# Low parts of the gate and up matrices: every piece, not every second one, by a second load that adds

## The chip, the core and the metric

The kernel runs on one core of a Trainium2 chip. TensorE (PE) does the matrix products, VectorE (DVE) and ScalarE (ACT) work on elements, GpSimd (POOL) and SyncE (SP) mostly issue DMAs here. 16 DMA engines move data between the chip's memory (DRAM) and the core's on-chip memory. DMAs issued by SP and by POOL stand in two different queues, q1 and q0 of the profile, and are served by the same 16 engines. The metric is device time of one execution in microseconds; lower is better.

## What is computed

One decoder layer over 256 tokens with 2048 channels, in float32: three token mixers, a SwiGLU block, a per-layer input embedding and a final norm. What matters here is the SwiGLU block:

```python
D_FF = -(-8 * D_MODEL // (3 * 256)) * 256        # 5632
...
        h = rms_norm(x, g_ffn[i])
        gate, up = jnp.split(h @ w_gate_up[i], 2, axis=-1)
        x = x + (jax.nn.silu(gate) * up) @ w_down[i]
```

The matrix `w_gate_up` has 2048 rows and 11264 columns, 92 MB in float32. It is used once, so the whole of it is streamed through the core.

## The kernel before

**Products in split form.** PE is fed with numbers of type float32r. To keep float32's accuracy, each operand is split in a high part (the value rounded to float32r) and a low part (the value less its high part), and each product is the sum of three: high by high, high by low, low by high (lines 255 to 257, function `products`). The tokens' side is split once; the weights are split as they arrive.

**Groups, chunks, pieces.** A `Group` is a block of 512 columns of one matrix with all its rows. `run(plan)` cuts it into `Chunk`s of 4 row blocks of 128, and a chunk has 2 pieces of 2 row blocks: 128 partitions by 2 by 512 numbers, 512 KB. Per piece PE does 2 row blocks by 2 halves of the tokens by 3 products: 12, so 24 for a chunk.

**Gate and up.** The plan has 11 column blocks `j`, for each a gate group and an up group of 16 row blocks, so 4 chunks each: 22 groups, 88 chunks, 176 pieces. They run in two parts, blocks 0 to 4 and blocks 5 to 10 (`CUT = 5`, line 964); after each part come the groups of `w_down` that use its results. Between chunks stand the evacuations: `ev_gate` (sigmoid on ACT, product on DVE), `ev_up` (product on DVE), and, two chunks later, the transposes of the result (line 324).

**The way of a piece.** `issue` (line 165) loads it into a buffer `raw` (a pool of 5) from SP. `split_w` makes its parts `whi` and `wlo` (pools of 5 each). It does so for the chunk after the one whose products come next in program order. For most pieces `split` copies `raw` to `whi` on ACT (line 111), rounding it, and subtracts on DVE: `wlo = raw - whi` (line 112). In the gate and up matrices the second piece of a chunk (`a == 1`) goes another way: ACT copies `raw` to `whi` (line 189) and writes the negated `whi` to `wlo` (line 190), and POOL issues a DMA (line 192) that loads the same 512 KB from DRAM a second time and adds it to `wlo` in place. So that piece is fetched twice, and DVE does nothing for it.

**What sets the order.** Each engine works through its own instructions in program order and waits on semaphores of the others. A piece's `whi` and `wlo` come free when PE has done the 12 products of the piece five before it. A `raw` buffer comes free when its last reader is done: DVE's subtraction, or ACT's copy where a second load is used. `c.ins` only places work of the mixers (`advance`), of which none is left in this stage.

Of the kernel before, what the change touches and what calls it, by code (L numbers as in the profile page):

```python
# [64 lines left out]
def kernel(  # L65
# [19 lines left out]
    def nm(s):  # L85
        uid[0] += 1
        return f"{s}_{uid[0]}"

    def big(name, shape=(P, 8, T), dt=F32):
        return t8.tile(list(shape), dt, tag="t8", name=nm(name))  # L90
# [19 lines left out]
    def split(hi, lo, src):  # L110
        a = act.activation(out=hi, in_=src, func=AF.Copy)  # L111
        b = dve.tensor_tensor(out=lo, in0=src, in1=hi.bitcast(F32), op=ALU.subtract)  # L112
        return a.ins, b.ins
# [59 lines left out]
    def split_w(c):  # L173
        c.parts = []
        if c.g.kind == "hold":
            b = big("whold", (P, 2, 4, c.g.n), F32R)
        for a, r in enumerate(c.raw):
            if c.g.kind == "hold":
                hi, lo = (b[:, q, 2 * a : 2 * a + 2, :] for q in range(2))
            else:  # L180
                hi = wparts.tile([P, 2, c.g.n], F32R, tag="whi", name=nm("whi"))
                lo = wparts.tile([P, 2, c.g.n], F32R, tag="wlo", name=nm("wlo"))
            if c is chunks[0]:
                for q in range(2):
                    c.g.pre([2 * a + q])
                    split(hi[:, q, :], lo[:, q, :], r[:, q, :])
            elif c.g.w is w_gu_v and a == 1:

                act.activation(out=hi, in_=r, func=AF.Copy)  # L189
                neg = act.activation(out=lo, in_=hi.bitcast(F32), func=AF.Copy, scale=-1.0)  # L190
                k = c.ks[2]
                nc.gpsimd.dma_start(  # L192
                    out=lo, in_=c.g.w[:, k : k + 2, c.g.c0 : c.g.c0 + c.g.n], accum_op=ALU.add
                )
                c.ins = (neg.ins, c.ins[1])
            else:
                c.ins = split(hi, lo, r)
            c.parts.append((hi, lo))
# [62 lines left out]
    def run(plan):  # L261
# [3 lines left out]
        while now[0] < len(chunks):  # L265
# [5 lines left out]
            while state["split"] < min(len(chunks), i + PREF_SPLIT):  # L271
                split_w(chunks[state["split"]])
                state["split"] += 1
# [77 lines left out]
    w_in_v, w_gu_v, w_dn_v = wv(w_in), wv(w_gate_up), wv(w_down)  # L351
# [757 lines left out]
```

## Time and profile before

| | us |
|---|---|
| median of 2 runs | 1913.3 (1912.48 to 1914.11) |
| the profiled execution, in all | 1915.16 |
| its span in the profile | 1913.4 |
| gate and up, first part (40 chunks) | 224.64 |
| `w_down`, first part | 109.7 |
| gate and up, second part (48 chunks) | 267.87 |

The profile shows one execution. Engines are named PE, PEld (PE's loading of the stationary operand, beside its products), DVE, ACT, POOL, SP. A group's row reads: line, engine, operation, output<-inputs, shape, count, then busy time and mean duration in ns of one, then the idle time just before them and who ended it. A row of the view of stretches reads: from:to, length, busy time and number of instructions of PE, PEld, DVE, ACT and POOL, then PE's granted clock (1.00 is full), the mean share of time in which the 16 DMA engines had a packet (above 1 where packets overlap), and GB/s. A row of a DMA queue reads: packets, MB, share of the 16 engines' time. A row of DMA issues ends with the median time in us from issue to landing. A row of waits reads: in total, how often, the longest. A row of the timeline reads: start, duration, engine, line, operation. A product's duration holds its way through the array; how fast PE goes is read from the distance of the starts.

### The profile page before, as it was taken

Reading aid. Unit: us, or ns where it says so; the run is one execution under the profiler, and the core shown is the slowest. Engines: PE = TensorE matmul, PEld = TensorE weight load, DVE = VectorE, ACT = ScalarE, POOL = GpSimd, SP = SyncE. Lnnn points to the kernel's source line nnn. Section 1 sums busy time; section 2 is a strip of 40 time slices with the busy share of each in tenths; the row PEclk is TensorE's granted clock in tenths of the full one; section 3 lists DMA queues with packets and bytes.
Section 4 is the critical chain, followed back from the end, with each engine's and each line's share of the span. In section 5 each row is a group of like instructions: output and inputs, shape, how many; then the busy total and the mean of one; then the engine's idle time right before and its main releaser. Section 6 shows DMA issues by size and latency. Waiting matters only on the chain.

```text
span 1913.4 us, 25619 instructions
## 1 busy us (share of the span) xinstructions
PE 1895.4 (99%) x9958; PEld 1633.6 (85%) x9958; DVE 1110.1 (58%) x1359; ACT 1001.5 (52%) x1122; POOL 115.0 (6%) x110
## 2 busy tenths in 40 slices
PE   8999999999999999999999999999999999999998
PEld 8988889999998888888888888888888888888887
DVE  8558776667888889765555332235433233355565
ACT  6466466544344444644445666653356666544554
POOL 1000000000000000000000122210012222100000
PEclk9999999999999999999999999999999999999999
DMA  8756556555666656676665999996699999966563
GB/s 276 219 168 199 175 176 185 161 156 172 179 185 198 193 165 211 194 239 188 209 191 185 255 289 275 275 280 193 191 262 284 277 288 280 274 187 191 183 187 122
DMA packets 213914, 407.41 MB, mean 213 GB/s; under 512 B 12976, under 2 KB 21808, under 8 KB 213664
## 3 DMA queue, kind: packets, MB, share of 16 engines
q1 hardware_dynamic: 188960, 356.02, 58.4%
q0 software_dynamic: 24832, 49.75, 14.6%
q8 instruction: 78, 1.28, 0.3%
q14 instruction: 44, 0.36, 0.1%
HBM read 403.62 MB, written 2.10 MB: 212 GB/s over the span
## 4 chain that ended last, share of the span: by engine, by line
PE 94%; DMA 3%; issue 1%; DVE 1%; ACT 0%; SPq 0%; POOLq 0%; DVEq 0%
PE acc L256 25%; PE acc L257 25%; PE acc L255 25%; PE acc L250 5%; PE acc L248 5%; PE acc L249 5%; DMA wlo<-in_w_gate_up_dram 2%; PE tr L324 1%; PE sc L546 1%; DMA x<-in_x_feat_dram 1%; DVE wlo L112 0%; DVE cv L105 0%; DMA raw<-in_w_in_dram 0%; DVE rw L734 0%; PE ov L617 0%
## 5 line engine op out<-in xcount | busy, mean ns | idle before, releaser
L112 DVE TENSOR_TENSOR wlo<-raw,whi 128x1024 fp32r<-128x1024 f32 (+2 forms) x590 | 705.7, 1199 | 694.0 <-ACT whi L111 693.2
L111 ACT ACTIVATE whi<-raw 128x1024 fp32r<-128x1024 f32 (+2 forms) x590 | 612.5, 1040 | 719.7 <-PE acc L257 508.9
L256 PE MATMUL acc<-wlo,xhi 128*128 128x512 f32 (+1 forms) x832 | 321.5, 386 | 2.2 <-DMA wlo<-in_w_gate_up_dram 2.1
L255 PE MATMUL acc<-whi,xhi 128*128 128x512 f32 (+1 forms) x832 | 321.3, 386 | 0.0
L257 PE MATMUL acc<-whi,xlo 128*128 128x512 f32 (+1 forms) x832 | 320.5, 385 | 0.0
L248 PE MATMUL acc<-hhi,whi 128*128 128x256 f32 x896 | 255.7, 285 | 5.3 <-ACT whi L111 5.1
L255 PE MATMUL acc<-whi,hhi 128*128 128x512 f32 (+1 forms) x672 | 255.6, 380 | 0.0
L250 PE MATMUL acc<-hhi,wlo 128*128 128x256 f32 x896 | 254.5, 284 | 0.9 <-DVE wlo L112 0.9
L257 PE MATMUL acc<-whi,hlo 128*128 128x512 f32 (+1 forms) x672 | 254.8, 379 | 0.0
L256 PE MATMUL acc<-wlo,hhi 128*128 128x512 f32 (+1 forms) x672 | 254.7, 379 | 0.0
L249 PE MATMUL acc<-hlo,whi 128*128 128x256 f32 x896 | 254.3, 284 | 0.0
L256 PEld LDWEIGHTS acc<-wlo,xhi 128*128 128x128 f32 x832 | 156.3, 188 | 36.7 <-DMA wlo<-in_w_gate_up_dram 6.1
L255 PEld LDWEIGHTS acc<-whi,xhi 128*128 128x128 f32 x832 | 156.3, 188 | 31.0
L257 PEld LDWEIGHTS acc<-whi,xlo 128*128 128x128 f32 x832 | 156.3, 188 | 30.8
L248 PEld LDWEIGHTS acc<-hhi,whi 128*128 128x128 f32 x896 | 172.8, 193 | 5.9 <-ACT whi L111 5.5
L250 PEld LDWEIGHTS acc<-hhi,wlo 128*128 128x128 f32 x896 | 172.6, 193 | 1.3 <-DVE wlo L112 1.3
L249 PEld LDWEIGHTS acc<-hlo,whi 128*128 128x128 f32 x896 | 172.9, 193 | 0.4 <-issue 0.2
L189 ACT ACTIVATE whi<-raw 128x1024 fp32r<-128x1024 f32 x88 | 93.3, 1061 | 134.1 <-PE acc L257 134.1
L257 PEld LDWEIGHTS acc<-whi,hlo 128*128 128x128 f32 x672 | 126.1, 188 | 23.6
L255 PEld LDWEIGHTS acc<-whi,hhi 128*128 128x128 f32 x672 | 126.2, 188 | 23.4
L256 PEld LDWEIGHTS acc<-wlo,hhi 128*128 128x128 f32 x672 | 126.2, 188 | 23.3
L192 POOL DMA_DIRECT2D wlo<-in_w_gate_up_dram x88 | 105.9, 1203 | 640.5 <-ACT wlo L190 583.1
(268 smaller groups left out, 2230.6 us busy)
## 6 DMA issues: line engine op xcount, KB each, us to landing
raw<-in_w_in_dram SPq DMA_DIRECT2D x262, 512.0 KB, 3.7
raw<-in_w_gate_up_dram SPq DMA_DIRECT2D x176, 512.0 KB, 5.9
wlo<-in_w_gate_up_dram POOLq DMA_DIRECT2D x88, 512.0 KB, 7.6
raw<-in_w_down_dram SPq DMA_DIRECT2D x88, 512.0 KB, 3.8
raw<-in_w_gla_out_dram SPq DMA_DIRECT2D x32, 512.0 KB, 3.7
raw<-in_w_o_dram SPq DMA_DIRECT2D x32, 512.0 KB, 3.7
raw<-in_w_ple_gate_dram SPq DMA_DIRECT2D x24, 512.0 KB, 4.1
raw<-in_w_sc_out_dram SPq DMA_DIRECT2D x16, 512.0 KB, 4.3
```

What stands on the lines that cost most here:

```text
L111: a = act.activation(out=hi, in_=src, func=AF.Copy)
L112: b = dve.tensor_tensor(out=lo, in0=src, in1=hi.bitcast(F32), op=ALU.subtract)
L189: act.activation(out=hi, in_=r, func=AF.Copy)
L192: nc.gpsimd.dma_start(out=lo, in_=c.g.w[:, k : k + 2, c.g.c0 : c.g.c0 + c.g.n], accum_op=ALU.add)
L248: pe.matmul(o, lhsT=whi[:, ms], rhs=shi, start=st and m % 2 == 0, stop=False)
L249: pe.matmul(o, lhsT=whi[:, ms], rhs=slo, start=False, stop=False)
L250: pe.matmul(o, lhsT=wlo[:, ms], rhs=shi, start=False, stop=sp and m % 2 == 1)
L255: pe.matmul(o, lhsT=shi[:, hs], rhs=whi, start=st, stop=False)
L256: pe.matmul(o, lhsT=shi[:, hs], rhs=wlo, start=False, stop=False)
L257: pe.matmul(o, lhsT=slo[:, hs], rhs=whi, start=False, stop=sp)
L324: pe.transpose(b[:, q, h * P : h * P + P], src[:, h, (j + q) * P : (j + q) * P + P], ident,)
L546: pe.matmul(b[:, e, :], lhsT=K[:, dt, :], rhs=Q[:, dt, :], start=q == 0, stop=q == 1)
```

## The change

The condition that picks the second piece of a chunk falls, so the first piece is made in the same way. The row block that the second load reads is now `c.ks[2 * a]`, 0 or 2 blocks into the chunk.

```diff
-            elif c.g.w is w_gu_v and a == 1:
+            elif c.g.w is w_gu_v:
 
                 act.activation(out=hi, in_=r, func=AF.Copy)
                 neg = act.activation(out=lo, in_=hi.bitcast(F32), func=AF.Copy, scale=-1.0)
-                k = c.ks[2]
+                k = c.ks[2 * a]
                 nc.gpsimd.dma_start(
                     out=lo, in_=c.g.w[:, k : k + 2, c.g.c0 : c.g.c0 + c.g.n], accum_op=ALU.add
                 )
-                c.ins = (neg.ins, c.ins[1])
+                c.ins = (neg.ins, neg.ins)
```

All else is as it was: the first load of every piece, the pools, the products. In 88 chunks one subtraction on DVE goes, and one copy on ACT and one DMA of 512 KB from POOL come.

ACT, some four chunks into the first part, before. The numbers behind the names tell buffers apart; DMAHW, DMASW, PE, DVE and Activation are the semaphores of SP's loads, of POOL's loads and of the engines:

```order
L111 ACTIVATE whi_9658<-raw_9617 128x1024 [waits DMAHW6_49,PE_49]
L189 ACTIVATE whi_9662<-raw_9619 128x1024 [waits DMAHW7_49,PE_49]
L190 ACTIVATE wlo_9663<-whi_9662 128x1024 [waits Activation_49]
L111 ACTIVATE whi_9700<-raw_9654 128x1024 [waits DMAHW0_49,PE_49]
L189 ACTIVATE whi_9704<-raw_9656 128x1024 [waits DMAHW1_49,DVE_49,PE_49]
L190 ACTIVATE wlo_9705<-whi_9704 128x1024 [waits DMASW0_49,Activation_49]
```

And now, at the same pieces:

```order
L189 ACTIVATE whi_9662<-raw_9620 128x1024 [waits DMAHW6_49,PE_49]
L190 ACTIVATE wlo_9663<-whi_9662 128x1024 [waits DMASW3_49,Activation_49]
L189 ACTIVATE whi_9667<-raw_9622 128x1024 [waits DMAHW7_49,PE_49]
L190 ACTIVATE wlo_9668<-whi_9667 128x1024 [waits DMASW4_49,Activation_49]
L189 ACTIVATE whi_9705<-raw_9658 128x1024 [waits DMAHW0_49,PE_49]
L190 ACTIVATE wlo_9706<-whi_9705 128x1024 [waits DMASW5_49,Activation_49]
L189 ACTIVATE whi_9710<-raw_9660 128x1024 [waits DMAHW1_49,PE_49]
L190 ACTIVATE wlo_9711<-whi_9710 128x1024 [waits DMASW6_49,Activation_49]
```

Three copies for a chunk have become four, and each negating copy also waits for the landing of an earlier second load, the one into the buffer that it writes.

SP, the loads at the same place, before:

```order
L165 DMA raw_9564<-in_w_gate_up_dram 128x2x512 [waits DMAHW0_49,DVE_49]
L165 DMA raw_9617<-in_w_gate_up_dram 128x2x512 [waits DMAHW1_49,Activation_49]
L165 DMA raw_9619<-in_w_gate_up_dram 128x2x512 [waits DMAHW2_49,DVE_49]
L165 DMA raw_9654<-in_w_gate_up_dram 128x2x512 [waits DMAHW3_49,Activation_49]
L165 DMA raw_9656<-in_w_gate_up_dram 128x2x512 [waits DMAHW4_49,DVE_49]
```

And now:

```order
L165 DMA raw_9566<-in_w_gate_up_dram 128x2x512 [waits DMAHW0_49,Activation_49]
L165 DMA raw_9620<-in_w_gate_up_dram 128x2x512 [waits DMAHW1_49,Activation_49]
L165 DMA raw_9622<-in_w_gate_up_dram 128x2x512 [waits DMAHW2_49,Activation_49]
L165 DMA raw_9658<-in_w_gate_up_dram 128x2x512 [waits DMAHW3_49,Activation_49]
L165 DMA raw_9660<-in_w_gate_up_dram 128x2x512 [waits DMAHW4_49,Activation_49]
```

The loads are the same in number and order; every one of them now waits for ACT to have read the buffer, none for DVE.

POOL, the first second loads of the stage, before:

```order
L192 DMA wlo_9479<-in_w_gate_up_dram 128x2x512 [waits DVE_49,DMASW0_49,PE_49,Activation_49]
L192 DMA wlo_9532<-in_w_gate_up_dram 128x2x512 [waits DVE_49,DMASW1_49,PE_49,Activation_49]
L192 DMA wlo_9571<-in_w_gate_up_dram 128x2x512 [waits DVE_49,DMASW2_49,PE_49,Activation_49]
L192 DMA wlo_9626<-in_w_gate_up_dram 128x2x512 [waits DVE_49,DMASW3_49,PE_49,Activation_49]
L192 DMA wlo_9663<-in_w_gate_up_dram 128x2x512 [waits DVE_49,DMASW4_49,PE_49,Activation_49]
```

And now:

```order
L192 DMA wlo_9475<-in_w_gate_up_dram 128x2x512 [waits DVE_49,DMASW0_49,PE_49,Activation_49]
L192 DMA wlo_9480<-in_w_gate_up_dram 128x2x512 [waits DVE_49,DMASW1_49,PE_49,Activation_49]
L192 DMA wlo_9529<-in_w_gate_up_dram 128x2x512 [waits DVE_49,DMASW2_49,PE_49,Activation_49]
L192 DMA wlo_9534<-in_w_gate_up_dram 128x2x512 [waits DVE_49,DMASW3_49,PE_49,Activation_49]
L192 DMA wlo_9569<-in_w_gate_up_dram 128x2x512 [waits DVE_49,DMASW4_49,PE_49,Activation_49]
```

Five of them reached into the fifth chunk before; now they reach into the third.

## The prediction

> **What bounds the kernel now.** I read the head of the page first, then the share of time by stage, then the waits, then the DMA queues in short windows. In the page's head and its forty slices:
>
> ```profile
> span 1913.4 us, 25619 instructions
> PE 1895.4 (99%) x9958; PEld 1633.6 (85%) x9958; DVE 1110.1 (58%) x1359; ACT 1001.5 (52%) x1122; POOL 115.0 (6%) x110
> PE   8999999999999999999999999999999999999998
> DMA  8756556555666656676665999996699999966563
> ```
>
> PE is busy 99% of the span, so the kernel is bound by PE. But the DMA row reads 9 in two places only, five slices and six slices long. These are the two parts of the gate-and-up stage, the only code the diff touches. The view of stretches, with a piece of the w_o stage ahead of it for comparison:
>
> ```profile
> core 0: us, PE busy (x) PEld busy (x) DVE busy (x) ACT busy (x) POOL busy (x), PEclk, DMA share, GB/s
> 1020.00:1067.70 47.70, 47.70 (x220) 39.67 (x219) 24.57 (x28) 25.95 (x35) 1.27 (x2) 1.00 0.65 187
> 1067.71:1292.35 224.64, 223.14 (x1002) 184.02 (x1000) 73.05 (x82) 140.26 (x147) 46.87 (x39) 1.00 1.05 280
> 1402.04:1669.91 267.87, 267.19 (x1193) 219.85 (x1192) 84.71 (x86) 163.14 (x165) 57.06 (x48) 1.00 1.05 283
> ```
>
> The borders are the first product that reads xhi and the first that reads aT. The two parts hold 5 and 6 column blocks of gate and up, 4 chunks for each of two groups: 40 and 48 chunks. So a chunk takes (224.64 + 267.87) / 88 = 5.60 us, and PE is busy for nearly all of it. The DMA share is 1.05 against 0.65 in w_o. A share above 1 means that packets overlap a little; whether 1.05 is a ceiling is the question that decides. Who waits for the second loads today:
>
> ```profile
> PE acc L256 <- DMA wlo<-in_w_gate_up_dram: 2.1, 4, 1.0
> PEld acc L256 <- DMA wlo<-in_w_gate_up_dram: 6.1, 10, 1.4
> wlo<-in_w_gate_up_dram POOLq DMA_DIRECT2D x88, 512.0 KB, 7.6
> raw<-in_w_gate_up_dram SPq DMA_DIRECT2D x176, 512.0 KB, 5.9
> ```
>
> **Is 1.05 the ceiling?** In this stage stretches with plain loads alone and with accumulating loads alone follow one another. Five of them, each 1.5 us long, from the view of stretches, and behind them the queue rows of 1105.0 to 1106.5 (q0) and 1107.5 to 1109.0 (q1):
>
> ```profile
> 1102.00:1103.50 1.50, 1.50 (x8) 1.25 (x7) 0.96 (x1) 0.51 (x1) 0.38 (x1) 1.00 1.05 397
> 1105.00:1106.50 1.50, 1.50 (x9) 1.23 (x8) 0.00 (x0) 1.29 (x2) 0.00 (x0) 1.00 1.16 214
> 1107.50:1109.00 1.50, 1.50 (x9) 1.23 (x8) 1.02 (x1) 0.45 (x1) 0.32 (x1) 1.00 1.05 400
> 1110.50:1112.00 1.50, 1.50 (x8) 1.23 (x8) 0.35 (x1) 1.23 (x2) 0.00 (x0) 1.00 1.09 206
> 1115.50:1117.00 1.50, 1.50 (x8) 1.24 (x7) 0.00 (x0) 1.47 (x2) 0.00 (x0) 1.00 1.13 208
> q0 software_dynamic: 155, 0.32, 115.0%
> q1 hardware_dynamic: 307, 0.60, 104.0%
> ```
>
> This is the row that decides. The share is the same either way, 1.05 to 1.16. Plain loads (q1, from SP) run at 400 GB/s, accumulating ones (q0, from POOL) at 206 to 214. An accumulating load occupies the 16 engines about twice as long per byte, and while it runs the plain ones get nearly nothing. So the engines are full, and their cost adds.
>
> For one transfer of 0.524 MB: a plain one costs 0.524/400 = 1.31 us. An accumulating one costs 0.524/209 = 2.51 us in mid-flight. Its start and its end, where the 16 engines are not all on it, come on top. That is bounded by longer windows, all time that isn't the plain loads' being put on it. The queue rows of 1080 to 1120 us, where DMA catches up, and of 1450 to 1650 us:
>
> ```profile
> q1 hardware_dynamic: 4208, 8.12, 55.1%
> q0 software_dynamic: 1912, 3.68, 51.9%
> q0 software_dynamic: 9753, 18.90, 54.9%
> q1 hardware_dynamic: 19300, 37.22, 50.2%
> ```
>
> The first pair is 15.5 plain and 7.0 accumulating transfers in 40 us: (40 - 15.5 x 1.31) / 7.0 = 2.81 us. The second is 71.0 and 36.0 in 200 us: 2.97 us, and this holds idle moments too. I take 2.75, between 2.51 and 2.81 and nearer the upper one, because that one holds starts and ends as the changed kernel will have them.
>
> Today a chunk needs 2 x 1.31 + 2.75 = 5.37 us of DMA against 5.60 us of PE: 96% full. That is why PE hardly waits though the stage stands at the ceiling.
>
> **The change, part by part.** In the 88 chunks the first piece's subtraction on DVE goes, and a negating copy on ACT, a DMA issue on POOL and 0.524 MB of accumulating traffic come. Rows of 1450 to 1650 us by line, and POOL's group from the page:
>
> ```profile
> L112 DVE TENSOR_TENSOR wlo<-raw,whi 128x1024 fp32r<-128x1024 f32 x35 | 42.9, 1226 | 113.5 <-ACT whi L111 113.5
> L190 ACT ACTIVATE wlo<-whi 128x1024 fp32r<-128x1024 f32 x36 | 38.2, 1061 | 1.1
> L192 POOL DMA_DIRECT2D wlo<-in_w_gate_up_dram x88 | 105.9, 1203 | 640.5 <-ACT wlo L190 583.1
> ```
>
> - DVE: 88 x 1.226 = 108 us less. DVE is busy 73.05 of 224.64 us there and PE never waits for it in these stages: worth 0.
> - ACT: 88 x 1.061 = 93 us more. It is busy 140.26 of 224.64 us over 40 chunks, 3.51 us a chunk; with 1.06 it is 4.57, still under PE's 5.60: 0. Behind the added copy on ACT stand the next piece's copy and the gate's sigmoid; both have that slack.
> - POOL: two issues of 1.203 us a chunk instead of one, 2.41 of 5.60 us: 0 by themselves.
> - SP: as many loads as before. A raw buffer now comes free at ACT's copy, about 1.2 us earlier for every second piece. That would help only if DMA had room; it has not: 0.
> - DMA: 2 x 1.31 + 2 x 2.75 = 8.12 us a chunk, above PE's 5.60. Its cover is gone, and this is the only term on the path: 88 x (8.12 - 5.60) = 222 us.
> - Against that, a head start. Five buffers let DMA work up to four pieces ahead, 4 x 2.72 = 10.9 us of PE time (half a chunk's 24 products, at the step below of 0.227 us), while the stage before still runs with a share of 0.65 of 1.05, 38% spare: 4.1 us, at two stage starts 8 us.
>
> Sum: 222 - 8 = +214 us. The profiled execution took 1915.2 us in all (span 1913.4), so 2129 us; the median of the runs is 1.9 us lower, which is nothing here. In the bounds: with 2.45 us (at 214 GB/s) a chunk is 7.52, +161, 2076 us. With 2.97 it is 8.56, +252, 2168. With the packets' own time in the 200 us window not corrected for overlap (54.9% x 200/36.0 = 3.05, 50.2% x 200/71.0 = 1.41) it is 8.92, +284, 2200.
>
> **A rule that speaks against it.** By bytes alone the chunk's four loads are 2.10 MB, at 400 GB/s 5.24 us, less than PE's 5.60; the sum would be 0. The Trainium skill, "DMA: Bandwidth & Descriptors" (Specifications), says with "Where 436 GB/s comes from" that for loads the HBM side binds, at about 358 GB/s for a core (it measures 425 with the pair's other core idle), and names no rate for an accumulating one; by the 358, as an estimate, a chunk would take 5.86 us and the kernel 1938 us. The trace does not agree with it at either end: plain loads reach 400 GB/s, and accumulating ones 209. I follow the rows.
>
> **The rivals.**
> - *Bytes count, not kind (not slower).* Place: the engines' share of 1.05. If a second accumulating load could fill time that the first leaves open, its added cost would shrink. It decides where an accumulating transfer costs no more than 5.60/2 - 1.31 = 1.49 us. Then 1915 us, at best 8 us less by the waits above. For it: today two accumulating loads hardly ever meet, so no row shows them together. Against it: with q0 alone the share is already 1.09 to 1.16.
> - *Partly so.* A transfer between 1.49 and 2.45 us; at 2.0 a chunk is 6.62 and the time 1915 + 90 - 8 = 1997 us.
> - *The buffers' circle, not the rate.* A piece's buffer is held for 2 x 1.06 us on ACT, the landing time L, and 2.72 us on PE; five pieces share it, so a piece takes (4.84 + L)/5. That passes 4.06 us (half of 8.12) when L is over 15.5 us. L is 7.6 now; with one accumulating and two plain loads ahead of it 7.6 + 2.75 + 2.62 = 13.0, not enough; with two ahead, 15.7, about equal; with three, 18.5, a piece takes 4.66 and the time is 1915 + 176 x (4.66 - 2.80) - 8 = 2234 us. For it: POOL's queue is in order. Against it: a longer L by queueing is DMA work being done, not a loss.
> - *PE's clock falls.* PE will wait some 1.3 us a piece. At the start of the kernel, the timeline shows products at half the step until 9.45 us, 4.3 us after the first:
>
> ```profile
> 9.03 0.41 PE L250 MATMUL acc<-hhi,wlo 128*128 128x256 f32 x1
> 9.24 0.41 PE L248 MATMUL acc<-hhi,whi 128*128 128x256 f32 x1
> 9.60 0.28 PE L250 MATMUL acc<-hhi,wlo 128*128 128x256 f32 x1
> 9.72 0.28 PE L248 MATMUL acc<-hhi,whi 128*128 128x256 f32 x1
> 1177.89 0.50 PE L256 MATMUL acc<-wlo,xhi 128*128 128x512 f32 x1 [1.03 <-DMA wlo<-in_w_gate_up_dram]
> 1178.46 0.39 PE L255 MATMUL acc<-whi,xhi 128*128 128x512 f32 x1
> 1178.69 0.40 PE L256 MATMUL acc<-wlo,xhi 128*128 128x512 f32 x1
> ```
>
> The step is 0.21 us there and 0.12 after. At half the rate a chunk's 24 products, now 0.23 us apart, take some 10.9 us: 88 x 5.3 = +466, 2381 us. Against it: after the wait of 1.03 us at 1177.89 the step stays 0.23. The Trainium skill, "TensorE: Matmul & The Clock Gate" (Part 1: The HAM clock gate), puts the fall after an idle window of about 3.4 us; by that rule these waits would be too short.
>
> **How the numbers follow.** DMA at its ceiling, 2075 to 2200 us: 0.78. Bytes alone, about 1915: 0.05. Partly so, 1930 to 2075: 0.07. The buffers' circle, of which half lies above 2200: 0.07. The clock: 0.03. The likeliest gives 2129 us; the range 2075 to 2200 is its own and takes in the bounds of both transfer prices, and with the lower half of the circle it holds about 0.8. Within 2% (38 us, about what a measurement can tell from no change) lie the bytes rival and the least of the partial one: 0.05. Faster by more than 2% I leave 0.01, since all waits that could go are 8 us. Slower: 0.94.
>
> **What would show it.** In the changed profile the two stages should be 88 chunks of about 8.1 us, some 320 and 385 us, with the DMA share still 1.05 to 1.1, while GB/s falls to about 260 (2.10 MB in 8.1 us). PE's waits at L256 for wlo should grow from 8 us to about 200, half of them at first pieces. Landing of wlo should pass 10 us. ACT, DVE and POOL should show the counts above and hold nobody. The stages behind, and the clock, should stay. I am wrong if GB/s rises above 300 in these stages, if the DMA share falls below 1 while PE waits, or if PE's granted clock leaves 1.00.

## The result and the profile after

The changed kernel takes 2132.7 us (median of two runs, 2131.33 and 2133.99) where the kernel before takes 1913.3. The ratio is 1.115, 95% interval 1.110 to 1.119: slower. The forecast was 2129 us, 2075 to 2200. The profiled execution took 2131.3 us with a span of 2129.6, 216.2 us more than the span before.

The head of the page and the forty slices, after:

```profile
span 2129.6 us, 25675 instructions
PE 1949.1 (92%) x9958; PEld 1625.1 (76%) x9958; DVE 1003.3 (47%) x1271; ACT 1093.0 (51%) x1210; POOL 220.1 (10%) x198
PE   8999999999999999999977777799777777789998
DMA  7756565556666666666699999966999999976653
```

The stage's two parts are the only slices where PE falls to 7, and the DMA row has its nines there as before. The parts by their own borders, with the piece of w_o ahead of them, in the view of stretches:

```profile
1020.00:1067.70 47.70, 47.70 (x220) 39.67 (x219) 21.75 (x26) 27.92 (x37) 3.64 (x3) 1.00 0.68 192
1068.30:1388.76 320.46, 247.32 (x1001) 179.73 (x1000) 27.26 (x44) 179.56 (x185) 92.18 (x77) 0.99 1.09 262
1498.45:1885.86 387.41, 296.92 (x1194) 215.74 (x1192) 29.17 (x40) 210.97 (x211) 111.93 (x94) 0.99 1.09 261
```

They took 224.64 and 267.87 us before: 95.8 and 119.5 us more, 215.4 together. So all but 0.8 us of the added span lies here. The DMA share is 1.09 against 1.05, while the rate fell from 280 to 262 GB/s: the engines are as busy as before and move fewer bytes in the same time. Who waits, and how long transfers are under way:

```profile
PE acc L256 <- DMA wlo<-in_w_gate_up_dram: 163.1, 161, 3.0
PEld acc L256 <- DMA wlo<-in_w_gate_up_dram: 235.3, 173, 3.5
raw<-in_w_gate_up_dram SPq DMA_DIRECT2D x176, 512.0 KB, 12.3
wlo<-in_w_gate_up_dram POOLq DMA_DIRECT2D x176, 512.0 KB, 14.7
```

PE waits for a second load at 161 of the 176 pieces, first and second ones alike; before, at 4. PE's own row shows 163 us and the stage grew by 215 (the row of PEld, which stands still before the same products, shows 235). The rest hides in what counts as busy: a product's duration of 0.39 us is counted whole, though the next one could start 0.23 us after it, and the first product behind a wait has a step of 0.33. That is some 0.16 + 0.10 us at each of 161 waits, 42 us, by this estimate most of the rest. Landing times doubled, for the plain loads too. The queues from 1560 to 1760 us:

```profile
q0 software_dynamic: 13556, 26.13, 70.4%
q1 hardware_dynamic: 13555, 26.13, 39.4%
```

In 200 us the engines moved 26.13 MB by each queue, 49.84 transfers of 0.5243 MB each. One accumulating and one plain load together cost 200 / 49.84 = 4.01 us, a chunk 8.03 us. With 1.31 us for the plain one, as the short windows before the change gave it, 2.70 us are left for the other.

### The profile page after: what moved, and what is told of

Its sections match the earlier page's. It is cut to its first block, busy times and chain, and to the rows that moved or that the text cites. A ratio compares the mean times of both kernels' runs of the same rounds, so it can differ in the third digit from the quotient of the medians.

```text
span 2129.6 us, 25675 instructions
## 1 busy us (share of the span) xinstructions
PE 1949.1 (92%) x9958; PEld 1625.1 (76%) x9958; DVE 1003.3 (47%) x1271; ACT 1093.0 (51%) x1210; POOL 220.1 (10%) x198
## 4 chain that ended last, share of the span: by engine, by line
PE 67%; DMA 30%; issue 1%; DVE 1%; ACT 0%; SPq 0%; POOL 0%; POOLq 0%; DVEq 0%
DMA wlo<-in_w_gate_up_dram 29%; PE acc L256 17%; PE acc L257 17%; PE acc L255 16%; PE acc L250 5%; PE acc L248 5%; PE acc L249 5%; PE tr L324 1%; PE sc L546 1%; DMA x<-in_x_feat_dram 0%; DVE wlo L112 0%; DMA raw<-in_w_in_dram 0%; DVE cv L105 0%; DVE rw L734 0%; POOL wlo L192 0%
## 5 line engine op out<-in xcount | busy, mean ns | idle before, releaser
L111 ACT ACTIVATE whi<-raw 128x1024 fp32r<-128x1024 f32 (+2 forms) x502 | 519.2, 1036 | 683.7 <-PE acc L257 476.1
L112 DVE TENSOR_TENSOR wlo<-raw,whi 128x1024 fp32r<-128x1024 f32 (+2 forms) x502 | 597.4, 1194 | 451.4 <-ACT whi L111 435.0
L256 PE MATMUL acc<-wlo,xhi 128*128 128x512 f32 (+1 forms) x832 | 342.7, 412 | 163.6 <-DMA wlo<-in_w_gate_up_dram 163.1
L189 ACT ACTIVATE whi<-raw 128x1024 fp32r<-128x1024 f32 x176 | 185.8, 1056 | 273.7 <-PE acc L257 272.5
L192 POOL DMA_DIRECT2D wlo<-in_w_gate_up_dram x176 | 210.9, 1200 | 745.5 <-ACT wlo L190 463.3
L105 DVE SCALAR_TENSOR_TENSOR ga<-acc,y,ga 128x512 f32<-128x512 f32 x44 | 31.5, 750 | 515.9 <-PE acc L257 271.9
L190 ACT ACTIVATE wlo<-whi 128x1024 fp32r<-128x1024 f32 x176 | 186.4, 1060 | 5.1
## 6 DMA issues: line engine op xcount, KB each, us to landing
wlo<-in_w_gate_up_dram POOLq DMA_DIRECT2D x176, 512.0 KB, 14.7
```

Of the source, the lines that this page charges most:

```text
L105: dve.scalar_tensor_tensor(out=o, in0=a, scalar=s, in1=b, op0=op0, op1=op1)
L192: nc.gpsimd.dma_start(out=lo, in_=c.g.w[:, k : k + 2, c.g.c0 : c.g.c0 + c.g.n], accum_op=ALU.add)
L256: pe.matmul(o, lhsT=shi[:, hs], rhs=wlo, start=False, stop=False)
```

## The experiments

Theory A is the forecast's: an accumulating load of 512 KB occupies the engines for about 2.7 us, a plain one for 1.3, and these times add. Against it stand B, bytes or transfers by number; C, the longer way of the first piece, a wait and not the engines' time; and D, a fixed cost for each accumulating transfer. Where no range is given, a measured time is that of a single execution; 13 executions of the kernel before, beside those of E1 to E4, lay between 1912.7 and 1917.5 us.

**E1, the second loads without the addition.** Leaves out the addition, so the low part is the weight itself.

```diff
                 nc.gpsimd.dma_start(
-                    out=lo, in_=c.g.w[:, k : k + 2, c.g.c0 : c.g.c0 + c.g.n], accum_op=ALU.add
+                    out=lo, in_=c.g.w[:, k : k + 2, c.g.c0 : c.g.c0 + c.g.n]
                 )
```

> The changed kernel, but every second load overwrites the low part instead of adding to it, so the addition is left out; same bytes, same number of transfers, same queue, same waits. Theory A (an accumulating transfer occupies the DMA engines for 2.7 us, a plain one 1.3 us, and these times add): a chunk needs 4 x 1.31 = 5.24 us of DMA, less than PE's 5.60, so about 1915 us (1905 to 1935). Theory B (the bytes, or the number of transfers on POOL's queue, set the time): about 2130 us. Theory C (the first piece's longer way through ACT, POOL and a late landing sets the time, not the engines' time): the way is the same, so 2050 to 2130 us. Should the change of type to float32r and not the addition be what slows the transfer, it also stays at about 2130 us.

Measured: 1914.4 us, against 1914.8 (the median) for the kernel before. The gate-and-up parts in the view of stretches, and the queues from 1160 to 1200 us:

```profile
1068.00:1292.00 224.00, 223.18 (x1005) 184.81 (x1004) 27.67 (x44) 179.68 (x186) 54.76 (x77) 1.00 1.15 370
1402.00:1670.00 268.00, 265.96 (x1192) 219.83 (x1191) 29.03 (x39) 210.42 (x211) 66.45 (x93) 1.00 1.16 372
q0 software_dynamic: 3927, 7.57, 65.0%
q1 hardware_dynamic: 3878, 7.47, 51.6%
```

All four loads of a chunk go through at 370 GB/s and PE is busy again. Same bytes, same 176 transfers, same queue, same change of type to float32r, same waits: only the addition is gone, and with it all of the added time. B falls, and the long way of C through ACT and POOL costs nothing by itself. The late landing is gone here too, so that part of C is left to E5.

**E2, the added traffic alone, first try.** The kernel before, with accumulating loads into buffers that are free in this stage (`sT`, `s10`, `gnb`), nobody reading them. (The lines that define the list `spare` of four such buffers are left out here, as are those that fill `last` in E5.)

```diff
             else:
                 c.ins = split(hi, lo, r)
+                if c.g.w is w_gu_v:
+                    for k in c.ks[:2]:
+                        spare.append(spare.pop(0))
+                        nc.gpsimd.dma_start(out=spare[0], in_=c.g.w[:, k, c.g.c0 : c.g.c0 + c.g.n], accum_op=ALU.add)
```

> The kernel before, plus the added traffic alone: for each first piece two accumulating loads of 256 KB into spare buffers that nobody reads, while DVE makes the low part as before. Nothing of the computation changes. Theory A: the engines have the same work as in the changed kernel, about 8.0 us a chunk, so about 2130 us (2090 to 2160), with PE waiting for loads whose own pieces were never changed. Theory C (the wait of the first piece is the price): that wait is not there, so about 1915 us (1910 to 1930).

Measured: 1969.0 us, which neither theory names. The slices show why:

```profile
PE   8999999999888998999999999999999999999998
POOL 1000001134443331000000012220012222100000
```

The loads depend on nothing in the stage, and they were set early, into the mixers' part of the program: POOL is busy in slices 7 to 16 (about 300 to 790 us), and PE has its dents there. So this run doesn't decide between A and C; it only shows that the same traffic costs 54 us in stages where DMA had room: in 300 to 787 us its share was 0.61 before and is 1.01 here.

**E5, the same traffic, tied to its place.** As E2, but each pair of spare loads is set behind the second load of the chunk before on POOL (`last[-1]`).

```diff
+                if c.g.w is w_gu_v and last:
+                    with tc.issue_after(last[-1]):
+                        for k in c.ks[:2]:
+                            spare.append(spare.pop(0))
+                            nc.gpsimd.dma_start(out=spare[0], in_=c.g.w[:, k, c.g.c0 : c.g.c0 + c.g.n], accum_op=ALU.add)
```

> The kernel before plus the added traffic alone, now tied to its place: the accumulating loads of 2 x 256 KB into spare buffers for a first piece stand on POOL right behind the second load of the chunk before (87 chunks). They add to float32 buffers, so no change of type is in them. DVE makes the low part of the first piece as before, nothing of the computation changes. Theory A (engine time adds: 2.7 us for an accumulating 512 KB): about 8.0 us a chunk, 2110 to 2140 us. Theory C (the price is the first piece's own wait for a late load): 1915 us. If adding without a change of type is cheaper: between, about 1914 + 87 x (2.6 + 2.7 + x - 5.6) for x us a 512 KB.

Measured: 2128.7 us. PE's waits, and a stretch that holds the first part:

```profile
PE acc L266 <- DMA wlo<-in_w_gate_up_dram: 143.6, 84, 3.0
1068.00:1390.00 322.00, 258.37 (x1012) 199.24 (x1011) 75.37 (x84) 141.38 (x148) 116.20 (x117) 0.93 1.10 263
```

The first piece is made on DVE as before the change, and PE waits at second pieces alone, 84 times: nothing that this kernel computes needs a load that the kernel before didn't have. The time is that of the changed kernel nevertheless, and so are the DMA share and the rate, 1.10 and 263 GB/s. C falls. The spare buffers are float32, so the price doesn't hang on the change of type either.

**E3, four buffers for the parts instead of five,** in the changed kernel.

```diff
-    wparts = ctx.enter_context(tc.tile_pool(name="wparts", bufs=5))
+    wparts = ctx.enter_context(tc.tile_pool(name="wparts", bufs=4))
```

> The changed kernel with 4 instead of 5 buffers for the parts. Theory A: DMA stays the bound; the landing time shrinks from 14.7 us to about 4 x 4.02 - 4.84 = 11.2 us because fewer transfers stand in the queue, and the time stays at 2130 to 2160 us. Theory C (the buffers' circle of 4.84 us plus a landing time of 14.7 us): a piece takes 19.5 / 4 = 4.9 us instead of 3.9 to 4.0, so 176 x 0.9 = 160 us more, about 2290 us.

Measured: 2137.2 us. First part and landing times:

```profile
1068.30:1388.80 320.50, 247.57 (x998) 180.31 (x997) 25.27 (x41) 181.31 (x187) 94.75 (x79) 0.99 1.09 262
raw<-in_w_gate_up_dram SPq DMA_DIRECT2D x176, 512.0 KB, 8.8
wlo<-in_w_gate_up_dram POOLq DMA_DIRECT2D x176, 512.0 KB, 10.7
```

The part is as long as with five buffers (320.46), and the second loads' landing fell from 14.7 to 10.7 us, where 11.2 was expected. Landing time here is a queue's length, which the buffers set; it isn't what the time hangs on.

**E4, no second loads at all,** the other end of the scale.

```diff
-            elif c.g.w is w_gu_v and a == 1:
+            elif False:
```

> The other direction: no second loads at all, both pieces' low parts by DVE. Theory A: a chunk needs 2.62 us of DMA, PE's waits of 8.2 us for second loads go, nothing else changes: 1905 to 1910 us, 0.2 to 0.4% below the kernel before. Rival: DVE's 1.23 us a piece, behind the evacuations of gate and up on the same engine, holds PE up somewhere: 1913 to 1930 us.

Measured: 1910.7 us (1910.4 to 1911.6 over 10 executions) against 1914.8; the ratio is 0.9978, 95% interval 0.9968 to 0.9987. The parts:

```profile
1068.00:1292.00 224.00, 224.00 (x1011) 185.90 (x1010) 121.08 (x123) 101.72 (x110) 0.00 (x0) 1.00 0.64 189
1402.00:1670.00 268.00, 268.00 (x1205) 222.34 (x1204) 141.71 (x133) 115.84 (x120) 0.55 (x1) 1.00 0.65 191
```

PE is busy without a break, DVE for 54% of the time and DMA at 0.64. This beats both kernels, the one before by 0.2%: little, but the interval lies clear of 1. The gain of 4 us is about half of the 8 us of waits, and the time lies just outside the 1905 to 1910 us that were expected. The subtraction that the second loads save DVE is hidden under PE anyway.

**E6, half of each piece by a second load,** the rest by DVE, all else as in the changed kernel.

```diff
-                neg = act.activation(out=lo, in_=hi.bitcast(F32), func=AF.Copy, scale=-1.0)
-                k = c.ks[2 * a]
+                neg = act.activation(out=lo[:, 1, :], in_=hi[:, 1, :].bitcast(F32), func=AF.Copy, scale=-1.0)
+                k = c.ks[2 * a] + 1
                 nc.gpsimd.dma_start(
-                    out=lo, in_=c.g.w[:, k : k + 2, c.g.c0 : c.g.c0 + c.g.n], accum_op=ALU.add
+                    out=lo[:, 1, :], in_=c.g.w[:, k, c.g.c0 : c.g.c0 + c.g.n], accum_op=ALU.add
                 )
+                tt(lo[:, 0, :], r[:, 0, :], hi[:, 0, :].bitcast(F32), ALU.subtract)
```

> The changed kernel, but the second load of each piece covers one of its two row blocks (256 KB), and DVE subtracts for the other; the result is the reference's. 176 accumulating transfers as in the changed kernel, and the bytes of the kernel before. Theory A (engine time by accumulating bytes): 5.37 us of DMA a chunk, under PE's 5.60: 1911 to 1925 us. Theory D (each accumulating transfer, or each POOL issue, costs a fixed time whatever its size): as the changed kernel, about 2130 us.

Measured: 1913.2 us, beside 1917.3 for a single execution of the kernel before. 176 accumulating transfers cost no more here than 88 when they carry half the bytes each: D falls, and the price goes by accumulated bytes.

**E7, the change for the gate groups alone.**

```diff
-            elif c.g.w is w_gu_v:
+            elif c.g.w is w_gu_v and (a == 1 or c.g.c0 < w_gu_v.shape[2] // 2):
```

> The changed kernel for the gate groups alone; the up groups as before. 132 accumulating loads instead of 88 or 176. Theory A with the numbers of the changed kernel's trace (8.03 us for a chunk with two, 5.37 for one with one, PE 5.60): a gate and an up group together need 53.6 us of DMA against 44.8 of PE, 11 x 8.8 = 97 us more, about 2011 us. If every added load simply cost the same wait: half of 216 us, 2022 us. If the up group's time let DMA catch up with nothing lost and lookahead were long: the same 2011; if the lookahead of five buffers is too short to use the slack in the up groups: nearer 2022.

Measured: 2012.6 us, where 2011 followed from the engine times and 2022 from an equal wait for every added load. The gap of 10 us between the two is small for one execution, but the trace has it too: from one gate group's first sigmoid to the next one's, a gate and an up group take 53.4 to 54.5 us, 53.5 in the median, where 53.6 follows from the engine times and 54.5 (4 x 8.03 + 4 x 5.60) if the up groups gave nothing back. So they did give back the little room that they have, 5.37 us of DMA under 5.60 of PE.

## Why the prediction was right

- *What bounds.* That a DMA share of 1.05 is the ceiling, and not a figure with room above it, carried the forecast. After, the share is 1.09 with PE waiting. The ceiling isn't one number: E1, with plain packets in both queues, runs at 1.15. What carried over, to 5%, was the rate of each kind in the short windows: by 400 and 209 GB/s one load of each takes 3.82 us, and 4.01 were measured.
- *DVE, ACT, POOL, SP at nothing.* Right: DVE 107 us less, ACT 92 more, POOL 105 more, and PE waits for none of them in this stage.
- *DMA, 222 us.* The chunk was put at 8.12 us and came to 8.03, so this term is 88 x (8.03 - 5.60) = 214 us, 8 less. The accumulating transfer cost 2.70 us, not 2.75. That the engines, kept busy from both queues, lose less at starts and ends than in the window of 1080 to 1120 us may be why; no run singles it out.
- *The head start, -8 us.* This step failed: nothing of it is left in the time. The two parts together, 707.9 us, are as long as 88 chunks of 8.03 us (706.6). DMA does start ahead: by the landing times in the trace, six plain loads of `w_gate_up` have landed when either part begins, 6 x 1.31 = 7.9 us of engine time. But the sum left out the other end, where SP already issues loads of `w_down`, which take engine time while PE still waits for the part's last pieces. In the view of DMA issues from 1372.8 to 1388.8 us, the last 16 us of the first part:

```profile
raw<-in_w_down_dram SPq DMA_DIRECT2D x4, 512.0 KB, 6.8
```

  The view counts the loads issued in this stretch; six loads of `w_down` land in it, three of them issued earlier, and six land in the last 16 us of the second part as well. So 7.9 us won at each start are given back at each end. This account is read from the trace; no run took those loads away. The two errors of the sum, 8 us too much for DMA and 8 us for a head start, cancelled, and that the forecast came within 4 us is luck to that extent.
- *Rivals.* Bytes alone: E1 shows that four plain loads a chunk are hidden and that adding is what isn't. By the limit of about 358 GB/s for a core that the Trainium skill, "DMA: Bandwidth & Descriptors" (Specifications), lists, E1 would be bound by DMA; its trace has 370 over whole parts, and PE is busy for 223.18 of 224 us. The 425 GB/s that the prediction quotes, for one core with the pair's other core idle, leave room for that. Partly so: with a second accumulating load in every chunk, one still costs 2.70 us, 2% below the figure that was taken and far above the 1.49 at which nothing would change. The buffers' circle: E3. PE's clock: it fell three times in the stage, for 3.4 us each, as told below. The parts are as long as the engines' time gives, so this cost next to nothing.
- *The signs named.* 8.1 us a chunk, parts of 320 and 385 us (320.46 and 387.41), rate 260 (262), landing above 10 us (14.7) all came. The stages behind stayed: `w_down` took 109.69 us after the first part in both kernels. PE's waits were to grow from 8 us, PE's and PEld's rows together, to about 200; PE's row has 163, for the reason above, and PEld's 235. The clock was to stay at 1.00, and leaving it was named as a sign of being wrong. It is 0.99 in the parts, and E5, where it is 0.93, takes no longer, so the clock isn't what sets the time.

## What to carry to other kernels

A load that adds to what lies on chip moves work from VectorE to the DMA engines and costs them about twice a plain load of the same bytes; count it in engine time, not in bytes, and against what DMA has left in that stage. Under a PE that is 99% busy, a high DMA share alone doesn't tell how much room is left: here a chunk had 0.23 us of room, and of the added 2.70 us the rest was paid in full, while E1 with a higher share was hidden. Look for short windows in which one kind of transfer runs alone, take its rate from there, and add up engine time. A long landing time can be only a queue's length: with four buffers instead of five it was a quarter shorter, and the time was the same.

## What the runs showed of the hardware that was not expected

The change of type in a transfer costs little or nothing: E1's loads, float32 to float32r from POOL, ran beside plain ones at 370 GB/s in all. From 1160 to 1200 us E1 moved 14.4 of them and 14.2 plain ones; with 1.31 us for a plain one, at most 1.48 us are left for one with the change, against 2.70 for one that adds. Why adding takes so long no run shows.

PE's clock fell after waits well under the 3.4 us of idleness that the prediction quoted from the Trainium skill, "TensorE: Matmul & The Clock Gate" (Part 1: The HAM clock gate). In the changed kernel, some rows of the timeline around 1186 us:

```profile
1183.69 0.39 PE L255 MATMUL acc<-whi,xhi 128*128 128x512 f32 x1
1185.88 0.50 PE L256 MATMUL acc<-wlo,xhi 128*128 128x512 f32 x1 [1.80 <-DMA wlo<-in_w_gate_up_dram]
1186.21 0.39 PE L257 MATMUL acc<-whi,xlo 128*128 128x512 f32 x1
1186.67 0.55 PE L256 MATMUL acc<-wlo,xhi 128*128 128x512 f32 x1
1187.44 0.63 PE L255 MATMUL acc<-whi,xhi 128*128 128x512 f32 x1
1187.87 0.63 PE L256 MATMUL acc<-wlo,xhi 128*128 128x512 f32 x1
1190.55 0.40 PE L257 MATMUL acc<-whi,xlo 128*128 128x512 f32 x1
1190.78 0.39 PE L255 MATMUL acc<-whi,xhi 128*128 128x512 f32 x1
```

After a wait of 1.80 us the step goes on at 0.23 us, turns to 0.43 some 0.9 us later, and is back at 0.23 after 3.4 us more. It isn't the length of one wait that decides. In the traces of the changed kernel, E3 and E5 the granted clock falls 37 times in these stages, each time for 3.41 us and each time a whole number of 3.41 us after the time before. Cut by that grid, the stages show what comes ahead of a fall. PE was idle for more than 0.533 of a stretch 36 times, and the next stretch had half the clock each time. Of all other stretches, some 700, only one was followed by a fall: the one that holds the wait of 1.80 us, idle for 0.527. So a window of the quoted length shows in the traces, but here it had to be idle for about half of its time, not all of it. In E5, where a wait comes once a chunk and is longer (1.7 us in the mean, against 1.0 in the changed kernel), 30 of the falls occur. Four stretches of E5:

```profile
1228.15:1231.56 3.41, 2.53 (x12) 1.75 (x10) 2.32 (x3) 2.31 (x3) 1.23 (x2) 1.00 1.10 263
1231.56:1234.97 3.41, 2.07 (x9) 1.72 (x10) 0.00 (x0) 1.06 (x1) 1.20 (x1) 1.00 1.10 264
1238.39:1241.80 3.41, 1.02 (x5) 0.67 (x4) 0.00 (x0) 2.11 (x2) 0.91 (x1) 1.00 1.11 264
1241.80:1245.21 3.41, 3.41 (x9) 2.64 (x8) 0.00 (x0) 0.00 (x0) 1.19 (x2) 0.50 1.10 263
```

A wait of 2.23 us that ends at 1232.90 is shared by the first two stretches, and the clock stays. One of 2.39 us that ends at 1241.03 lies in the third alone, and the fourth has half the clock. The granted clock of the whole run is 0.975, and it takes no longer than the changed kernel with its three falls: here the slower products filled time in which PE would have waited. What they would cost where PE sets the pace no run here shows.
